# Softmax over 32,768 columns on one core: the last tile in one load and four pieces, the tile before it stored ahead

## The chip, the core and the metric

The kernel runs on one core of a Trainium2 chip. The core has engines that run side by side, each with its own instruction queue: VectorE (DVE in the profile) for maxima, sums and scalings, ScalarE (ACT) for exponentials, and SyncE (SP), which here only issues transfers. Transfers between main memory and the on-chip memory run on 16 DMA engines; a transfer is issued by SP, which uses queue q1, or by ScalarE, which uses queue q10. The metric is device time in microseconds (us). The kernel before takes 2502.16 us, the median of three runs (2502.09 to 2502.26).

## The reference

```python
scaled = logits / temperature                      # logits: 16 x 256 x 32768, float32; temperature 1.0
scaled = scaled - scaled.max(axis=-1, keepdims=True)
exp_scaled = np.exp(scaled)
return exp_scaled / exp_scaled.sum(axis=-1, keepdims=True)
```

It is a softmax over each of 4096 rows of 32,768 numbers. Input and output are 537 MB each.

## The kernel before

Each row is split into 4 parts of 8192 columns (`_SPLIT`), and a part lies on one partition. So a tile of 128 partitions holds 32 whole rows, as 128 x 8192 float32 (4 MB), and there are G = 128 tiles, 0 to 127. Six buffers of that size hold tiles in turn (`_BUFS`); everything is done in place in the buffer.

For a tile, five steps follow each other:

- `load` (L57, issued at L60 by SP): from main memory into the buffer. Tiles 0 and 127 come in two halves of 4096 columns (`cuts`, L53, `_END_CUT`), all others in one transfer.
- `peaks` (L82): VectorE takes the negated maximum of each partition (L88; with two halves, the smaller of the two at L92). `combine` (L69) then joins the four partitions of a row: two rounds of a shuffle within 32 partitions (L72) and an operation of one column (L75).
- `exps` (L101): ScalarE computes exp(x - maximum) in place and adds up each partition as it goes (L107).
- `scales` (L116): VectorE joins the sums of the four partitions (`combine` again), takes the reciprocal (L125) and multiplies the tile by it (L127).
- `store` (L64, issued at L67): back to main memory. ScalarE issues the stores of tiles 0 to 125, SP those of 126 and 127; tile 127 is stored in two halves.

The order is written out by hand (`manual_schedule`, L131 to L143); each engine executes its instructions in that order. Six loads are issued ahead. Then, for each i, `peaks(i+1)` and `exps(i+1)` come before `scales(i)` and `store(i)`, and after these the load of tile i+6 into the buffer that tile i leaves. That load has to wait until the store of tile i has landed. At the end this means: `peaks(127)` stands ahead of `scales(126)` on VectorE.

Of the kernel before, what the change touches and what calls it, by code (L numbers as in the profile page):

```python
# [1 line left out]

# [4 lines left out]


_SPLIT = 4
_BUFS = 6  # L10
_END_CUT = 4096


@with_exitstack
def kernel(
    ctx: ExitStack,
    tc: tile.TileContext,
    logits: bass.AP,
    temperature: bass.AP,
    out: bass.AP,  # L20
):
    nc = tc.nc
    inv_t = 1.0 / float(temperature)
    P = nc.NUM_PARTITIONS
    fp32 = mybir.dt.float32
    Exp = mybir.ActivationFunctionType.Exp
    X = mybir.AxisListType.X
    A = mybir.AluOpType

    xf = logits.flatten_outer_dims()  # L30
    of = out.flatten_outer_dims()
    N, V = xf.shape
    W = V // _SPLIT
    assert W * _SPLIT == V and (N * _SPLIT) % P == 0
    x = xf.rearrange("n (h v) -> (n h) v", h=_SPLIT)
    o = of.rearrange("n (h v) -> (n h) v", h=_SPLIT)
    G = N * _SPLIT // P
    R = _SPLIT.bit_length() - 1

    pool = ctx.enter_context(tc.tile_pool(name="fixed", bufs=1))  # L40
    bufs = [pool.tile([P, W], fp32, name=f"x{b}") for b in range(_BUFS)]
    stats = [
        (
            pool.tile([P, 4], fp32, name=f"pk{b}"),
            pool.tile([P, 4], fp32, name=f"sm{b}"),
            pool.tile([P, R + 1], fp32, name=f"mx{b}"),
            pool.tile([P, R + 1], fp32, name=f"su{b}"),
            pool.tile([P, 1], fp32, name=f"rs{b}"),
        )
        for b in range(4)  # L50
    ]

    def cuts(i: int) -> list[tuple[int, int]]:  # L53
        step = _END_CUT if i in (0, G - 1) else W
        return [(s, step) for s in range(0, W, step)]

    def load(i: int) -> None:  # L57
        xs = bufs[i % _BUFS]
        for s, n in cuts(i):
            nc.sync.dma_start(  # L60
                out=xs[:, s : s + n], in_=x[i * P : (i + 1) * P, s : s + n]
            )

    def store(i: int, eng) -> None:  # L64
        xs = bufs[i % _BUFS]
        for s, n in cuts(i) if i == G - 1 else [(0, W)]:
            eng.dma_start(out=o[i * P : (i + 1) * P, s : s + n], in_=xs[:, s : s + n])  # L67

    def combine(v, op) -> None:  # L69
        for j in range(R):  # L70
            mask = [k ^ (1 << j) for k in range(32)]
            nc.vector.stream_shuffle(  # L72
                out=v[:, j + 1 : j + 2], in_=v[:, j : j + 1], mask=mask
            )
            nc.vector.tensor_tensor(  # L75
                out=v[:, j + 1 : j + 2],
                in0=v[:, j : j + 1],
                in1=v[:, j + 1 : j + 2],
                op=op,
            )  # L80

    def peaks(i: int) -> None:  # L82
        xs = bufs[i % _BUFS]
        pk, _, mx, _, _ = stats[i % 4]
        cs = cuts(i)
        to = [mx[:, 0:1]] if len(cs) == 1 else [pk[:, k : k + 1] for k in range(len(cs))]
        for (s, n), t in zip(cs, to):
            nc.vector.tensor_reduce(  # L88
                out=t, in_=xs[:, s : s + n], axis=X, op=A.max, negate=True
            )  # L90
        if len(cs) > 1:
            nc.vector.tensor_reduce(  # L92
                out=mx[:, 0:1], in_=pk[:, : len(cs)], axis=X, op=A.min
            )
        combine(mx, A.min)
        if inv_t != 1.0:
            nc.vector.tensor_scalar_mul(
                out=mx[:, R : R + 1], in0=mx[:, R : R + 1], scalar1=inv_t
            )

    def exps(i: int) -> None:  # L101
        xs = bufs[i % _BUFS]
        _, sm, mx, su, _ = stats[i % 4]
        cs = cuts(i)
        to = [su[:, 0:1]] if len(cs) == 1 else [sm[:, k : k + 1] for k in range(len(cs))]
        for (s, n), t in zip(cs, to):
            nc.scalar.activation(  # L107
                out=xs[:, s : s + n],
                in_=xs[:, s : s + n],
                func=Exp,  # L110
                bias=mx[:, R : R + 1],
                scale=inv_t,
                accum_out=t,
            )

    def scales(i: int) -> None:  # L116
        xs = bufs[i % _BUFS]
        _, sm, _, su, rs = stats[i % 4]
        cs = cuts(i)
        if len(cs) > 1:  # L120
            nc.vector.tensor_reduce(  # L121
                out=su[:, 0:1], in_=sm[:, : len(cs)], axis=X, op=A.add
            )
        combine(su, A.add)
        nc.vector.reciprocal(out=rs, in_=su[:, R : R + 1])  # L125
        for s, n in cs:
            nc.vector.tensor_scalar_mul(  # L127
                out=xs[:, s : s + n], in0=xs[:, s : s + n], scalar1=rs
            )

    with tc.manual_schedule():  # L131
        for i in range(_BUFS):
            load(i)
        peaks(0)
        exps(0)
        for i in range(G):
            if i + 1 < G:
                peaks(i + 1)
                exps(i + 1)
            scales(i)  # L140
            store(i, nc.scalar if i < G - 2 else nc.sync)
            if i + _BUFS < G:
                load(i + _BUFS)  # L143


# [1 line left out]
_INS = ['logits', 'temperature']  # L147
_OUTS = [((16, 256, 32768), 'float32')]

_NUMBERS = {'temperature': 1.0}  # L150


# [26 lines left out]
```

## Time and profile before

| what | value |
|---|---|
| median of the runs | 2502.16 us |
| the profiled execution: its own time | 2501.61 us |
| its span, from the first instruction to the end | 2499.8 us |
| bytes read / written | 536.87 MB / 536.87 MB |
| VectorE idle, waiting for loads (L88, tiles in one load) | 564.1 us |
| L88, maximum of 128x8192 | 8686 ns each |
| L107, exponential, 130 instructions | 7017 ns each (mean of two sizes) |
| L127, scaling, 130 instructions | 4421 ns each (mean of two sizes) |
| 4 MB load by SP, issue to landing | 38.5 us (median of 126) |
| 4 MB store by ScalarE, issue to landing | 43.4 us (median of 126) |

The span is the profiler's; the execution's own time is 1.8 us longer and is what compares with the runs. "Landing" is the moment at which a transfer's last part has arrived. A busy engine counts only instructions that compute: waiting and issuing transfers are not in it. A line such as `ACTq L67 DMA_DIRECT2D` is the issue of a transfer, not the transfer itself. Times in windows, timeline and chain run from the start of the span.

### The profile page before, as it was taken

To read this page: it belongs to the slowest core of one execution; us is meant where nothing else is said; L and a number is where in the kernel's file an instruction comes from. 1 tells how busy PE (TensorE), PEld (TensorE's weight loads), DVE (VectorE), ACT (ScalarE), POOL (GpSimd) and SP (SyncE) were. 2 spreads that over 40 slices of the span, in tenths; PEclk is the share of its full clock that TensorE was granted. 3 is DMA by queue.
4 is the path that set the end of the run, shared out by engine and by line. 5 is a ranking of instruction groups with operands and counts; after the bars stand their busy time and mean duration, and the time that the engine had idled before them with its cause. 6 is when DMAs were issued, how large, how long until landed. Compare 5 with 4: busy or idle time off the path is not lost.

```text
span 2499.8 us, 2866 instructions
## 1 busy us (share of the span) xinstructions
DVE 1857.8 (74%) x1928; ACT 925.3 (37%) x261; POOL 0.2 (0%) x4
## 2 busy tenths in 40 slices
DVE  7877777777777777777677776777777777777765
ACT  3433433334333433334333343333433344333432
POOL 0000000000000000000000000000000000000000
DMA  9999999999999999999999999999999999999997
GB/s 411 432 435 433 433 433 434 433 433 434 434 431 434 434 433 433 434 433 432 433 435 432 433 434 433 432 433 434 433 433 433 433 432 433 435 432 434 434 431 317
DMA packets 37318, 1073.94 MB, mean 430 GB/s; under 512 B 4144, under 2 KB 4144, under 8 KB 4144
## 3 DMA queue, kind: packets, MB, share of 16 engines
q1 hardware_dynamic: 19152, 545.27, 50.6%
q10 hardware_dynamic: 18144, 528.49, 49.0%
q14 instruction: 22, 0.18, 0.0%
HBM read 536.87 MB, written 536.87 MB: 430 GB/s over the span
## 4 chain that ended last, share of the span: by engine, by line
DMA 83%; DVE 15%; ACT 1%; issue 0%; DVEq 0%; SPq 0%; ACTq 0%
DMA out_dram<-x 43%; DMA x<-in_logits_dram 40%; DVE mx L88 9%; DVE x L127 4%; ACT x L107 1%; DVE mx L72 0%; DVE su L75 0%; DVE su L72 0%; DVE mx L75 0%; DVE pk L88 0%; DVE rs L125 0%; DVEq L174 0%; SPq L60 0%; DVE su L121 0%; DVE mx L92 0%
## 5 line engine op out<-in xcount | busy, mean ns | idle before, releaser
L88 DVE TENSOR_REDUCE mx<-x 128x1 f32<-128x8192 f32 x126 | 1094.4, 8686 | 564.1 <-DMA x<-in_logits_dram 564.1
L107 ACT ACTIVATE x<-x,mx 128x8192 f32<-128x8192 f32 (+1 forms) x130 | 912.2, 7017 | 1546.5 <-DVE su L72 1469.8
L127 DVE TENSOR_SCALAR x<-x,rs 128x8192 f32<-128x8192 f32 (+1 forms) x130 | 574.5, 4421 | 4.5
L75 DVE TENSOR_TENSOR su<-su 128x1 f32<-128x1 f32 x256 | 40.9, 160 | 8.8
L75 DVE TENSOR_TENSOR mx<-mx 128x1 f32<-128x1 f32 x256 | 40.9, 160 | 8.8
L72 DVE STREAM_SHUFFLE su<-su 128x1 f32<-128x1 f32 x256 | 38.8, 151 | 0.0
L72 DVE STREAM_SHUFFLE mx<-mx 128x1 f32<-128x1 f32 x256 | 38.8, 151 | 0.0
L88 DVE TENSOR_REDUCE pk<-x 128x1 f32<-128x4096 f32 x4 | 17.7, 4418 | 18.5 <-DMA x<-in_logits_dram 18.5
L125 DVE RECIPROCAL rs<-su 128x1 f32<-128x1 f32 x128 | 21.0, 164 | 4.5
L107 ACT ACTIVATION_READ_ACCUMULATOR x<-x,mx 128x1 f32 x130 | 24.2, 186 | 0.0
L72 DVE LOAD_MASK_SELECT mx<-mx x256 | 3.6, 14 | 11.0
L72 DVE LOAD_MASK_SELECT su<-su x256 | 3.6, 14 | 5.6
L107 ACT ACT_TABLE_LOAD x1 | 1.3, 1283 | 8.2 <-DMA x<-in_logits_dram 8.2
L121 DVE TENSOR_REDUCE su<-sm 128x1 f32<-128x2 f32 x2 | 0.3, 151 | 2.2 <-ACT x L107 2.2
L92 DVE TENSOR_REDUCE mx<-pk 128x1 f32<-128x2 f32 x2 | 0.3, 155 | 0.1
L160 POOL MEMSET const-bfloat16-1.0<- 128x1 bf16 x1 | 0.1, 102 | 0.0
L160 POOL MEMSET const-uint8-127<- 128x1 uint8 x1 | 0.1, 102 | 0.0
L160 POOL MEMSET const-float32-0.0<- 128x1 f32 x1 | 0.1, 99 | 0.2 <-issue 0.2
L160 POOL MEMSET const-float32-1.0<- 128x1 f32 x1 | 0.1, 99 | 0.0
## 6 DMA issues: line engine op xcount, KB each, us to landing
x<-in_logits_dram SPq DMA_DIRECT2D x126, 4096.0 KB, 38.5
out_dram<-x ACTq DMA_DIRECT2D x126, 4096.0 KB, 43.4
x<-in_logits_dram SPq DMA_DIRECT2D x4, 2048.0 KB, 22.7
out_dram<-x SPq DMA_DIRECT2D x1, 4096.0 KB, 11.2
out_dram<-x SPq DMA_DIRECT2D x2, 2048.0 KB, 11.6
```

Source lines behind the costliest of these rows:

```text
L72: nc.vector.stream_shuffle(out=v[:, j + 1 : j + 2], in_=v[:, j : j + 1], mask=mask)
L75: nc.vector.tensor_tensor(out=v[:, j + 1 : j + 2], in0=v[:, j : j + 1], in1=v[:, j + 1 : j + 2], op=op,)
L88: nc.vector.tensor_reduce(out=t, in_=xs[:, s : s + n], axis=X, op=A.max, negate=True)
L92: nc.vector.tensor_reduce(out=mx[:, 0:1], in_=pk[:, : len(cs)], axis=X, op=A.min)
L107: nc.scalar.activation(out=xs[:, s : s + n], in_=xs[:, s : s + n], func=Exp, bias=mx[:, R : R + 1], scale=inv_t, accum_out=t,)
L121: nc.vector.tensor_reduce(out=su[:, 0:1], in_=sm[:, : len(cs)], axis=X, op=A.add)
L125: nc.vector.reciprocal(out=rs, in_=su[:, R : R + 1])
L127: nc.vector.tensor_scalar_mul(out=xs[:, s : s + n], in0=xs[:, s : s + n], scalar1=rs)
L160: nc = _bacc.Bacc("TRN2", target_bir_lowering=False, num_devices=1)
```

## The change

Four edits, all at the end of the kernel:

- Tile 127 is loaded in one transfer. Tile 0 keeps its two halves.
- `scales(126)` and `store(126)` come before anything is computed on tile 127. The loop ends at tile 126, and a new function `finish(127)` follows it.
- `finish` works in four pieces of 2048 columns. Each piece has its own maximum, and its exponential uses that maximum alone, so it need not wait for the maximum of the whole row. Afterwards the overall maximum is formed, with `combine`; a small exponential `ee` (128 x 4) gives the factor by which each piece is off; one instruction multiplies these factors by the four sums and adds them up; `combine`, the reciprocal and a small multiplication give a factor `f` for each piece. Then each piece is scaled and stored by itself: four stores of 1 MB.
- ScalarE issues all stores, those of tiles 126 and 127 included.

```diff
-_END_CUT = 4096
+_FIRST_CUT = 4096
+_LAST_CUT = 2048
...
+    last = [pool.tile([P, W // _LAST_CUT], fp32, name=nm) for nm in ("ee", "f", "tt")]
+
     def cuts(i: int) -> list[tuple[int, int]]:
-        step = _END_CUT if i in (0, G - 1) else W
+        step = {0: _FIRST_CUT, G - 1: _LAST_CUT}.get(i, W)
         return [(s, step) for s in range(0, W, step)]
 
     def load(i: int) -> None:
         xs = bufs[i % _BUFS]
-        for s, n in cuts(i):
+        for s, n in cuts(i) if i == 0 else [(0, W)]:
...
-    def store(i: int, eng) -> None:
+    def store(i: int) -> None:
         xs = bufs[i % _BUFS]
         for s, n in cuts(i) if i == G - 1 else [(0, W)]:
-            eng.dma_start(out=o[i * P : (i + 1) * P, s : s + n], in_=xs[:, s : s + n])
+            nc.scalar.dma_start(
+                out=o[i * P : (i + 1) * P, s : s + n], in_=xs[:, s : s + n]
+            )
...
+    def finish(i: int) -> None:
+        xs = bufs[i % _BUFS]
+        nm, sm, mx, su, rs = stats[i % 4]
+        ee, f, tt = last
+        cs = cuts(i)
+        for k, (s, n) in enumerate(cs):
+            nc.vector.tensor_reduce(
+                out=nm[:, k : k + 1], in_=xs[:, s : s + n], axis=X, op=A.max, negate=True
+            )
...
+            nc.scalar.activation(
+                out=xs[:, s : s + n],
+                in_=xs[:, s : s + n],
+                func=Exp,
+                bias=nm[:, k : k + 1],
+                scale=inv_t,
+                accum_out=sm[:, k : k + 1],
+            )
+        nc.vector.tensor_reduce(out=mx[:, 0:1], in_=nm, axis=X, op=A.min)
+        combine(mx, A.min)
+        nc.scalar.activation(out=ee, in_=nm, func=Exp, bias=mx[:, R : R + 1], scale=-1.0)
+        nc.vector.tensor_tensor_reduce(
+            out=tt,
+            in0=ee,
+            in1=sm,
+            scale=1.0,
+            scalar=0.0,
+            op0=A.mult,
+            op1=A.add,
+            accum_out=su[:, 0:1],
+        )
+        combine(su, A.add)
+        nc.vector.reciprocal(out=rs, in_=su[:, R : R + 1])
+        nc.vector.tensor_scalar_mul(out=f, in0=ee, scalar1=rs)
+        for k, (s, n) in enumerate(cs):
+            nc.vector.tensor_scalar_mul(
+                out=xs[:, s : s + n], in0=xs[:, s : s + n], scalar1=f[:, k : k + 1]
+            )
+
     with tc.manual_schedule():
...
-        for i in range(G):
-            if i + 1 < G:
+        for i in range(G - 1):
+            if i + 2 < G:
                 peaks(i + 1)
                 exps(i + 1)
             scales(i)
-            store(i, nc.scalar if i < G - 2 else nc.sync)
+            store(i)
             if i + _BUFS < G:
                 load(i + _BUFS)
+        finish(G - 1)
+        store(G - 1)
```

## The prediction

> **What bounds the kernel now.** I read the page first: busy times, DMA line, chain shares.
>
> ```profile
> DVE 1857.8 (74%) x1928; ACT 925.3 (37%) x261; POOL 0.2 (0%) x4
> DMA packets 37318, 1073.94 MB, mean 430 GB/s; under 512 B 4144, under 2 KB 4144, under 8 KB 4144
> DMA 83%; DVE 15%; ACT 1%; issue 0%; DVEq 0%; SPq 0%; ACTq 0%
> ```
>
> No engine is full, and 83% of the chain is transfers: the kernel moves 1,074 MB and is bound by that. The change touches only the end, so next I cut the end into stretches by window (columns: DVE busy, ACT busy, POOL busy, clock, DMA share, GB/s).
>
> ```profile
> 2300.00:2450.00 150.00, 113.16 (x120) 52.90 (x15) 0.00 (x0) 1.00 1.00 433
> 2450.00:2463.00 13.00, 7.23 (x2) 4.82 (x2) 0.00 (x0) 1.00 0.96 412
> 2463.00:2478.00 15.00, 10.39 (x16) 5.45 (x3) 0.00 (x0) 1.00 0.09 37
> 2478.00:2498.00 20.00, 5.56 (x10) 2.05 (x2) 0.00 (x0) 1.00 0.98 419
> ...
> 2470.00:2471.00 1.00, 1.00 (x1) 0.00 (x0) 0.00 (x0) 1.00 0.08 33
> ```
>
> From 2463 to 2478 the DMA engines look idle: 15 us that an early store could fill. But they are not quite idle. Full rate is 433 GB/s, or 433/16 = 27.1 GB/s for one of the 16 engines; 33 to 37 GB/s is about one engine's worth. So I asked who that is, from the time to landing of the last stores and loads (DMA issues, one window per answer), with issue times from the timeline and the chain.
>
> ```profile
> out_dram<-x ACTq DMA_DIRECT2D x1, 4096.0 KB, 38.5
> ...
> out_dram<-x ACTq DMA_DIRECT2D x1, 4096.0 KB, 33.7
> ...
> out_dram<-x ACTq DMA_DIRECT2D x1, 4096.0 KB, 23.8
> ...
> out_dram<-x SPq DMA_DIRECT2D x1, 2048.0 KB, 13.0
> ```
>
> Issued at 2414.25, 2433.57, 2452.93 and (the last half) 2485.89, these landed at 2452.75 (tile 123), 2467.27 (124), 2476.73 (125) and 2498.9 (127). A landing is complete when the last engine has done its part. Between 123 and 124, 14.52 us passed, in which one store (4.19 MB) and one half load of tile 127 (2.10 MB) landed: 6.29 MB / 16 / 14.52 us = 27.1 GB/s, exactly one engine's full rate. Between 124 and 125: 4.19 MB / 16 / 9.46 us = 27.7 GB/s. So one engine, some 10 us behind the others, never rests until 2476.73, and it alone makes the landings late. The 15 us belong to the other engines; the late one rests only from 2476.7 until the store of tile 126, issued at 2477.93, reaches it, and the two last stores then take 2498.9 - 2477.9 = 21.0 us. **The bound at the end is this one engine's remaining bytes, plus its rest.** It also explains the chain here:
>
> ```profile
> 2419.30 47.81 DMA x<-in_logits_dram
> 2467.11 0.02 issue
> 2467.14 4.43 DVE pk L88
> ```
>
> Tile 127's second half lands at 2467.1, 29.1 us after tile 126 (2438.06), where the step is 19.35. The queues' packets say why:
>
> ```profile
> q10 hardware_dynamic: 191, 5.67, 65.6%
> q1 hardware_dynamic: 193, 2.95, 34.4%
> ```
>
> From 2425 to 2445 both queues get equal numbers of packets, but those of the half loads hold half the bytes (16 KB against 32 KB), so loads get a third of the rate.
>
> **The change, part by part.**
>
> *One load for tile 127.* Packets are 32 KB again and the queues share equally, as they do all through (19.35 us a tile). The load lands at 2438.06 + 19.4 = 2457.5, not 2467.1. No bytes are saved: what the load gains, the stores beside it lose, so this is worth nothing to the late engine by itself. One SP issue (0.33 us) goes; nothing waits for it.
>
> *Tile 126 ahead.* Its exponential's accumulator is read by 2454.63 + 0.18 = 2454.8. VectorE takes 0.96 us from there to the scaling (2480.28 to 2481.24 in the same sequence), then 4.49: done at 2460.3 instead of 2477.9. The first-half maximum that filled 2452.8 to 2457.2 is gone. ScalarE issues the store at about 2460.4. What waits behind it on ScalarE is tile 127's first exponential, which needs a maximum not ready before 2462.6, so the wait costs nothing. On the late engine this store stands behind those of 124 and 125, still queued until about 2476.7. It therefore starts at 2476.7 without a rest: 4.19 MB at 433 GB/s is 9.69 us, so it lands at 2486.4 (before: 2477.93 + 11.2 = 2489.1). On the others it fills the idle 15 us, worth nothing.
>
> *Tile 127.* Four maxima of 128x2048: the rows of 8192 (8,686 ns) and 4096 (4,418) give 2.13 us per 2048, so 2.28 each, 9.1 together, from 2460.3 to 2469.4. Exponentials (3.70 for 4096, 7.12 for 8192) come to 2.0 each and keep pace; the last is read by 2471.7. The overall minimum and its combine (0.96, from 2471.59 to 2472.55) hide beside it. The small exponential `ee` has no row: between the accumulator read (0.19) and a whole 2048 piece (2.0), I take 0.3 from the line through the two sizes, so 2472.0. The multiply-and-sum has none either: between 0.16 (an add of one column) and 2.3 (a 2048 maximum); 0.3 with its gap, near the small row: 2472.3. Combine and reciprocal 0.96, `f` 0.2: 2473.5. Scaling pieces 1.2 each (4.62 for two halves): the first store issues at 2474.7, the last at 2478.3. All of it has cover: the late engine needs tile 127 only at 2486.4, 11 us after. With both upper bounds (3.7 more) and a load still landing at 2467.1 (6.8 more) it would be 2485.2, still in time. So the added small instructions cost nothing.
>
> *Four stores of 1 MB.* The two halves landed at 2483.60 + 10.3 = 2493.9 and 2498.9; from the store before (2489.1) that is 9.8 us for 4.19 MB, against 9.69 at full rate. Halving cost 0.1. For quarters I take 0.2: landing at 2486.4 + 9.9 = 2496.3. Bounds: nothing (2496.1), and 4.5 if each of the three cuts leaves the whole gap of a start on empty queues (11.2 - 9.69 = 1.5 us); 0.2 lies by the row that is nearest, a cut with another transfer queued ahead.
>
> The Trainium skill speaks against this part: "DMA: Bandwidth & Descriptors", section "Measured (HBM→SBUF, 128 partitions, SWDGE, issued from GpSimd)", gives 6.15 us and 78% of the rate to a transfer of 1 MB, and advises at least that size. Taken one after the other, four would be 24.6 us by it, an estimate that lands tile 127 at 2511.0 and makes the kernel 12 us slower. The two halves above show no such price where another transfer is queued ahead, and I go by them; no run here shows quarters yet.
>
> *All stores on ScalarE.* 126 and 127 move from SP's queue to ScalarE's. Before, both queues were empty by then; now 126 follows 125 on one queue. Five issues of 0.34 us on an idle ScalarE; SP only waits at the end.
>
> **Sum.** Last landing 2498.9 → 2496.3, 2.6 us, of which the rest on the late engine is all. Call it 2.5. The span ends 0.9 us after the last landing in both: 2497.3. The profiled execution took 2501.61, 1.8 more than its span; so 2499.1. The median shown is 0.55 above that execution: **2499.6 us**, 0.1% faster. This measurement can tell about 0.2% (5.0 us) from no change, so that counts as no change. With quarters at nothing and the faster of the two paces seen (9.46 instead of 9.69, twice) it would be 2498.9; with a gap at each cut 2503.9.
>
> **Rivals.**
> - *The idle 15 us are real for the end* (the lag dissolves, or the late engine is not one engine). For it: a DMA share of 0.09. Then tile 127's arithmetic sets the end: first issue 2474.7, and 11.2 from issue to landing of 4 MB on empty queues gives 2486, 13 us earlier: 2489. Against it: the two rates of 27.1 and 27.7 GB/s. Chance 0.09.
> - *Quarters are too small a transfer (slower).* If a quarter takes as long as a half (4.9 us), tile 127 needs 19.5 and lands at 2505.9: 2509. It decides from 3.1 us a piece (12.3 us for the four, all of the gain), and passes 0.2% at 4.3. Against it: halving cost 0.1. Chance 0.04.
> - *Nothing comes of it*: the late engine finds another gap of 2 us, at the change from 125 to 126 or from 126 to 127, so that the change does not do what it says: 2502. For it: every start on empty queues shows such a gap; against it: both stores are queued 10 us ahead. Chance 0.09.
> - My forecast: 0.78, with 2498.9 to 2503.9 as its own range.
>
> Faster by over 0.2% is the first rival, 0.09; slower the second, 0.04; the rest, 0.87, is within. The range is the forecast's, which takes in the third rival: with 0.3 below for the rounding of the views, 2498.6 to 2503.9.
>
> **What would show it.** Right: tile 127's load lands near 2457.5; the store of 126 issues near 2460.4 and lands near 2486.4, some 26 us later; first store of 127 issued near 2475, last landing near 2496.3; from 2473 on the DMA share falls towards one engine's until tile 127's pieces come, and at the very end again a stretch of some 10 us at about 30 GB/s, with the others done. Wrong: tile 126 landing 11 us after its issue, or all engines busy until the end.

## The result and the profile after

The changed kernel takes 2498.40 us, the median of 20 runs (2498.23 to 2499.61); the kernel before took 2502.10 beside it (20 runs, 2500.97 to 2503.39). The ratio is 0.9986, with a 95% interval of 0.998 to 0.9993. So it is 3.7 us faster, 0.15%, where 2.5 us were forecast: less than 0.2%, as forecast, but 0.2 us below the lower end of the range. The profiled execution took 2498.68 us, with a span of 2496.9 us.

The first three lines are from the page of the changed kernel; the others are its end cut into stretches (DVE busy, ACT busy, POOL busy, clock, DMA share, GB/s).

```profile
DVE 1858.4 (74%) x1934; ACT 926.4 (37%) x266; POOL 0.2 (0%) x4
DMA packets 37462, 1073.94 MB, mean 430 GB/s; under 512 B 4160, under 2 KB 4160, under 8 KB 4160
DMA 83%; DVE 15%; ACT 1%; issue 0%; SPq 0%; DVEq 0%; ACTq 0%
```

```profile
2450.00:2463.00 13.00, 10.86 (x11) 5.27 (x3) 0.00 (x0) 1.00 0.98 421
2463.00:2473.00 10.00, 8.17 (x21) 7.81 (x9) 0.00 (x0) 1.00 0.98 423
2473.00:2485.00 12.00, 4.45 (x4) 0.00 (x0) 0.00 (x0) 1.00 0.87 365
2485.00:2496.00 11.00, 0.00 (x0) 0.00 (x0) 0.00 (x0) 1.00 0.09 37
...
2486.00:2487.00 1.00, 0.00 (x0) 0.00 (x0) 0.00 (x0) 1.00 0.12 49
...
2492.00:2493.00 1.00, 0.00 (x0) 0.00 (x0) 0.00 (x0) 1.00 0.06 25
```

The page is all but the same. In the windows, the stretch at 0.09 and 37 GB/s has not gone: it stood at 2463 to 2478, and now it stands at 2485 to 2496, at the very end. From 2486 on no more than two engines work (0.12 is two sixteenths), and from 2490 on one alone (0.06, 25 GB/s); the others are done. The stores of tiles 126 and 127 say the same, first their issues in the timeline:

```profile
2460.05 0.34 ACTq L70 DMA_DIRECT2D out_dram<-x  x1
...
2473.90 4.02 ACTq L70 DMA_DIRECT2D out_dram<-x  x4
```

and their time to landing, for tile 126 and for the last quarter of 127 (DMA issues by window):

```profile
out_dram<-x ACTq DMA_DIRECT2D x1, 4096.0 KB, 26.0
...
out_dram<-x ACTq DMA_DIRECT2D x1, 1024.0 KB, 18.4
```

Tile 126 was issued at 2460.05 and landed 26.0 us later, at 2486.05: more than twice the 11.2 us of before, although it left 18 us sooner. The last quarter of tile 127, issued at 2477.5, landed at 2495.9. Everything waits in the queue of one engine. Tile 126's line of before, from the page, and the rest of the late engine there, a window in which no packet starts, with the same window in the changed kernel:

```profile
out_dram<-x SPq DMA_DIRECT2D x1, 4096.0 KB, 11.2
...
2476.40:2478.70 2.30, 1.50 (x1) 2.30 (x1) 0.00 (x0) 1.00 0.00 0
...
2476.40:2478.70 2.30, 1.05 (x1) 0.00 (x0) 0.00 (x0) 1.00 0.98 406
```

### The profile page after: what moved, and what is told of

It reads as the page before. It is cut to its first block, busy times and chain, and to the rows that moved or that the text cites. A ratio compares the mean times of both kernels' runs of the same rounds, so it can differ in the third digit from the quotient of the medians.

```text
span 2496.9 us, 2877 instructions
## 1 busy us (share of the span) xinstructions
DVE 1858.4 (74%) x1934; ACT 926.4 (37%) x266; POOL 0.2 (0%) x4
## 4 chain that ended last, share of the span: by engine, by line
DMA 83%; DVE 15%; ACT 1%; issue 0%; SPq 0%; DVEq 0%; ACTq 0%
DMA out_dram<-x 43%; DMA x<-in_logits_dram 40%; DVE mx L93 9%; DVE x L132 4%; ACT x L112 1%; DVE pk L142 0%; DVE su L80 0%; DVE mx L77 0%; DVE su L77 0%; DVE mx L80 0%; DVE rs L130 0%; DVE x L174 0%; ACT x L149 0%; SPq L63 0%; DVEq L223 0%
## 5 line engine op out<-in xcount | busy, mean ns | idle before, releaser
L77 DVE STREAM_SHUFFLE su<-su 128x1 f32<-128x1 f32 x256 | 38.8, 152 | 0.0
L77 DVE STREAM_SHUFFLE mx<-mx 128x1 f32<-128x1 f32 x256 | 38.8, 151 | 0.0
L93 DVE TENSOR_REDUCE pk<-x 128x1 f32<-128x4096 f32 x2 | 8.8, 4420 | 8.6 <-DMA x<-in_logits_dram 8.6
L149 ACT ACTIVATE x<-x,pk 128x2048 f32<-128x2048 f32 x4 | 8.0, 2002 | 8.0 <-DVE pk L142 7.7
L142 DVE TENSOR_REDUCE pk<-x 128x1 f32<-128x2048 f32 x4 | 8.9, 2278 | 0.0
## 6 DMA issues: line engine op xcount, KB each, us to landing
x<-in_logits_dram SPq DMA_DIRECT2D x127, 4096.0 KB, 38.5
out_dram<-x ACTq DMA_DIRECT2D x127, 4096.0 KB, 43.4
```

Source lines behind the costliest of these rows:

```text
L77: nc.vector.stream_shuffle(out=v[:, j + 1 : j + 2], in_=v[:, j : j + 1], mask=mask)
L93: nc.vector.tensor_reduce(out=t, in_=xs[:, s : s + n], axis=X, op=A.max, negate=True)
L142: nc.vector.tensor_reduce(out=nm[:, k : k + 1], in_=xs[:, s : s + n], axis=X, op=A.max, negate=True)
L149: nc.scalar.activation(out=xs[:, s : s + n], in_=xs[:, s : s + n], func=Exp, bias=nm[:, k : k + 1], scale=inv_t, accum_out=sm[:, k : k + 1],)
```

## The experiments

**Which edit does it?** Two kernels carry one edit each.

`load_only`, the kernel before with tile 127 in one load:

```diff
-        for s, n in cuts(i):
+        for s, n in cuts(i) if i == 0 else [(0, W)]:
```

> The kernel before with one edit: tile 127 loaded in one transfer. Theory (the rest of one late DMA engine before the store of tile 126 is the whole gain): the load lands near 2457, tile 126 is scaled by 2472 and its store issued before the late engine is empty (2476.7), so nearly the whole gain comes: 2498.4 to 2498.9 us, as much as the full change. Rival 1 (the idle time of all 16 engines counts): the store of tile 126 is issued 6 us sooner, so 2496. Rival 2 (part of the 3.7 us comes from the stores moved to ScalarE or from the four pieces): about 2499.5, as only the 2.5 us of the forecast are the rest.

Measured: 2498.25 us (11 runs), ratio 0.9986 (0.9978 to 0.9995).

`early_only`, the kernel before with tile 126 scaled and stored ahead of everything on tile 127:

```diff
         for i in range(G):
-            if i + 1 < G:
+            if i == G - 1:
+                peaks(i)
+                exps(i)
+            if i + 2 < G:
                 peaks(i + 1)
                 exps(i + 1)
             scales(i)
```

> The kernel before with one edit: tile 126 scaled and stored ahead of everything on tile 127; the load in two halves, tile 127 in two halves with one maximum, and the stores of 126 and 127 on SP stay. Theory: the store of tile 126 is issued near 2460.4 and the first half of tile 127 near 2483.6, both before the late engine needs them (2476.7 and 2486.4), so nearly the whole gain again: 2498.4 to 2498.9 us; the gains of the two edits do not add. Rival 1 (idle time of all engines counts): 2490 or less. Rival 2 (part of the gain from ScalarE's stores or the four pieces): about 2499.5.

Measured: 2498.43 us (11 runs), ratio 0.9987 (0.9978 to 0.9995). The three last stores of `load_only` in the timeline, and the time to landing of the first of them, tile 126:

```profile
2472.99 8.29 SPq L67 DMA_DIRECT2D out_dram<-x  x3
```

```profile
out_dram<-x SPq DMA_DIRECT2D x1, 4096.0 KB, 13.8
```

The same in `early_only`:

```profile
2460.25 25.90 SPq L67 DMA_DIRECT2D out_dram<-x  x3
```

```profile
out_dram<-x SPq DMA_DIRECT2D x1, 4096.0 KB, 26.1
```

Tile 126 was issued 12.7 us apart in the two, and landed at 2486.8 and 2486.35. Each edit alone gives the whole gain, since either one puts a store into the late engine's queue before it is empty, and more than that it can't use. Rival 1 (idle time of all engines) is out. So is rival 2: without ScalarE's stores and without the four pieces the gain is just as large, so `finish` and the move of the stores add nothing to it that these runs can tell.

**Does tile 127's arithmetic have the 11 us of cover?** Idle maxima of 128x8192 were put ahead of it, one in `delay_9` (`range(1)`), two in `delay_17`, whose edit is shown; nothing reads their result:

```diff
+    idle = pool.tile([P, 1], fp32, name="idle")
...
+        for _ in range(2):
+            nc.vector.tensor_reduce(
+                out=idle, in_=bufs[(G - 3) % _BUFS], axis=X, op=A.max, negate=True
+            )
         finish(G - 1)
```

> The changed kernel with one idle maximum of 128x8192 (8.7 us on VectorE) ahead of tile 127's work. Theory: the first store of tile 127 is issued near 2482.6 instead of 2473.9, still ahead of the late engine's need at 2486.0, so no change: 2498.4 us, within 0.5. Rival 1 (tile 127's arithmetic sets the end): 8.7 us more, 2507.

> The changed kernel with two idle maxima of 128x8192 (17.4 us on VectorE) ahead of tile 127's work. Theory: the first store is issued near 2491.3, the late engine is empty at 2486.0 and rests some 6 us, so 2504.0 to 2505.0 us. Rival 1 (tile 127's arithmetic sets the end): 17.4 us more, 2515.8.

Measured: 2498.56 us for one (10 runs; 8.7 us of added work cost 0.2, which is within the scatter; the first store of tile 127 was issued at 2482.23, ahead of tile 126's landing), and 2506.31 for two (10 runs; ratio to the kernel before 1.0017, 1.0008 to 1.0026), 1.3 above the theory's range. In `delay_17` the windows show a true rest:

```profile
2473.00:2485.00 12.00, 12.00 (x5) 4.53 (x5) 0.00 (x0) 1.00 0.10 44
2485.00:2492.00 7.00, 5.17 (x20) 4.03 (x5) 0.00 (x0) 1.00 0.00 0
2492.00:2504.00 12.00, 3.48 (x3) 0.00 (x0) 0.00 (x0) 1.00 0.84 350
```

First one engine's stretch (0.10), then nothing at all (0.00), then all engines together. The first quarter was issued at 2491.93 and landed 3.9 us later, 10.2 us after tile 126 (2460.76 + 24.8 = 2485.6), where the changed kernel needs 2.4 from one to the other: a rest of 7.8 us for 17.4 us of added work. The theory expected 6: it left out the 1.5 us that a start on empty queues takes beyond the transfer (11.2 less 9.69, for tile 126 in the kernel before).

**Why 3.7 us between medians, and 2.9 between the profiles?** The kernel before was profiled again, without any edit.

> The kernel before once more, for a second profile. Open: medians differ by 3.7 us, the two profiles by 2.9. Theory: the rest of the late engine varies by about one 32 KB packet (1.2 us) between executions, with the order in which its packets of tile 127's load and of the stores alternate. Then an execution of about 2502.2 us shows a longer step from the landing of store 125 to that of store 126 than the 12.3 us of the first profile (12.8 to 13.5), and one of about 2501.1 a shorter or equal one. Rival: the step is 12.3 in all executions and the time differs in the earlier part, so that the landing of tile 126's load moves with the time.

> As before_b, a third profile of the kernel before: theory and rival as there.

Measured: 2500.93 and 2501.48 us. The steps from the landing of store 125 to that of 126 were 12.4 and 12.5 us; the first profile's is 12.4 from the same rows, each rounded to 0.1 us (the expectation has it as 12.3). The rest did not vary here; the times differed earlier, by the landing of tile 126's load. That is what the rival expected, and neither execution was one of 2502. So the next three profiles went after one:

> The kernel before, a fourth profile. Open: why the medians differ by 3.7 us where the rest of the late engine in three profiles is 2.7 (125 to 126 in 12.3 to 12.5 us). Three profiles of before took 2500.9 to 2501.6, below the median of 2502.1. Theory of the phase: on the late engine packets of loads and stores alternate, and which queue is ahead differs by one packet between executions (in delay_17 the store of tile 122 landed 2.4 us ahead of the load of tile 126, in the other profiles 0.2 after it). The kernel before ends a fixed time after the load of tile 127, so it is later when stores are ahead; the changed one ends when the late engine's total is done, in either phase. So an execution near 2502.2 has the load of tile 126 landing near 2438.4, the store of 122 some 2.4 us ahead of it, and 125 to 126 in 13.5 or more; one near 2501.2 looks like the first three. Rival: the store lands 0.2 us after the load in a 2502.2 execution as well.

> The kernel before, a fifth profile. The theory of the phase and its rival expect here what they expect of before_d.

> The kernel before, a sixth profile. The theory of the phase and its rival expect here what they expect of before_d.

> The changed kernel, a second profile. Theory of the phase: 2498.2 to 2498.9 us in either phase, with store 125 to 126 in 9.7 us; if the stores are ahead here, the load of tile 126 lands some 1 us later than in the first profile (2437.7) and the time is no later for it. Rival: a later landing of that load is a later end by as much.

Measured: 2502.32, 2500.93, 2500.88, and 2498.27 for the changed kernel. `before_d` is the execution looked for. Its page (issues, with the median time to landing) has

```profile
x<-in_logits_dram SPq DMA_DIRECT2D x126, 4096.0 KB, 41.1
out_dram<-x ACTq DMA_DIRECT2D x126, 4096.0 KB, 40.7
```

where the other five profiles of before have 38.5 to 38.8 and 43.0 to 43.4. In the median the loads land 2.6 us later and the stores 2.7 us sooner. The last tiles show the order directly: the store of tile 122 landed at 2395.59 + 40.7 = 2436.3, 2.5 us ahead of the load of tile 126 (2438.77); in the first profile it landed 0.2 after it (2438.28 and 2438.06). The stores are ahead on the late engine, by about the time of a packet of each kind (two times 1.21 us, an estimate from 32 KB at 27.1 GB/s). At the end of `before_d`, in the timeline and then in the times to landing of the stores of 125 and 126:

```profile
2453.65 0.34 ACTq L67 DMA_DIRECT2D out_dram<-x  x1
2467.83 4.42 DVE L88 TENSOR_REDUCE pk<-x 128x1 f32<-128x4096 f32 x1 [9.89 <-DMA x<-in_logits_dram]
2478.63 0.35 SPq L67 DMA_DIRECT2D out_dram<-x  x1
```

```profile
out_dram<-x ACTq DMA_DIRECT2D x1, 4096.0 KB, 22.6
...
out_dram<-x SPq DMA_DIRECT2D x1, 4096.0 KB, 11.2
```

Tile 127 is there 0.7 us later than in the first profile (2467.1), but store 125 lands 0.5 us sooner, at 2476.25. Tile 126 lands at 2489.83: 13.6 us from one to the other, so by this sum the engine rests 3.9 us where it rested 2.7 (the step less the 9.69 of the transfer). The stretch in which no packet starts is longer by as much, 3.5 us against 2.3 in the windows:

```profile
2475.90:2479.40 3.50, 2.70 (x1) 3.50 (x3) 0.00 (x0) 1.00 0.00 0
```

The second profile of the changed kernel, `after_b`, happened to have the same order:

```profile
x<-in_logits_dram SPq DMA_DIRECT2D x127, 4096.0 KB, 41.1
out_dram<-x ACTq DMA_DIRECT2D x127, 4096.0 KB, 40.7
```

and in its timeline tile 126's maximum, which starts when the load has landed:

```profile
2438.57 8.69 DVE L93 TENSOR_REDUCE mx<-x 128x1 f32<-128x8192 f32 x1 [4.50 <-DMA x<-in_logits_dram]
```

Its tile 126 arrived 0.8 us later than in the first profile after (2437.76), and it ended 0.4 us sooner, 2498.27 against 2498.68. This is what the theory of the phase expected, and against its rival. The span of the kernel before ends 32.7 to 32.8 us after tile 127's load in all six profiles; the changed kernel ends when the late engine has moved all its bytes, in whatever order.

**Can the late engine be relieved?** In `late_15`, tile 127 is stored as 120 partitions and 8:

```diff
+            for a, b in [(0, 120), (120, P)] if i == G - 1 else [(0, P)]:
+                nc.scalar.dma_start(
+                    out=o[i * P + a : i * P + b, s : s + n], in_=xs[a:b, s : s + n]
+                )
```

> The changed kernel, with each of tile 127's four stores as two: 120 partitions and 8 partitions. Theory: the end is the late engine's queue alone. 120 partitions divide over 15 engines and not 16. If the engine left out is the late one, its last bytes are those of tile 126 (landing 2486.0) and the second latest engine sets the end, some 5.5 us earlier: 2492.5 to 2494.5 us. If another engine is left out, the late one has as much or a ninth row more per store: 2498.4 to 2499.7. Rival 1 (all engines' rate sets the end): 16/15 of 9.7 us, 0.6 more: 2499.0.

Measured: 2506.08 us (11 runs), ratio 1.0018 (1.0009 to 1.0027), slower by more than any theory had it. The issues of its last stores in the timeline, and by window the stretch in which they are under way and two of its last microseconds:

```profile
2474.05 19.70 ACTq L71 DMA_DIRECT2D out_dram<-x  x8
```

```profile
2475.00:2493.00 18.00, 2.61 (x3) 0.00 (x0) 0.00 (x0) 1.00 0.79 228
...
2495.00:2496.00 1.00, 0.00 (x0) 0.00 (x0) 0.00 (x0) 1.00 0.08 33
...
2503.00:2504.00 1.00, 0.00 (x0) 0.00 (x0) 0.00 (x0) 1.00 0.06 25
```

One engine still moves alone up to 2504, so it was not the late one that was left out. Issuing eight stores took 19.7 us, where four took 4.0, and the rate between 2475 and 2493 stayed between 139 and 311 GB/s in windows of 1 us. The engines were busy for much of that time, but moved less in it: a share of 0.79 gave 228 GB/s, where in the changed kernel 0.87 gave 365. Why this split is so slow was not found; with that the experiment says nothing on what relief of the right engine would bring.

**When does the engine fall behind?** `half_run` leaves out tiles 64 to 127:

```diff
-    G = N * _SPLIT // P
+    G = N * _SPLIT // P // 2
```

> The changed kernel on the first 64 tiles alone (tiles 64 to 127 are left out, half of the work). Theory of a slow drift (the late engine falls behind evenly over the run): the stretch at the end in which only one engine or two still move data is about half as long as in the full run (11 us from 2485 to 2496), 5 to 6 us, and the time is about 1251 to 1255 us. Rival (the late engine loses its 10 us once, at the start or at the end): the stretch stays near 10 us.

Measured: 1253.09 us (one execution).

```profile
1233.00:1244.00 11.00, 0.00 (x0) 0.00 (x0) 0.00 (x0) 1.00 0.91 384
1244.00:1250.00 6.00, 0.00 (x0) 0.00 (x0) 0.00 (x0) 1.00 0.08 34
```

The stretch in which one or two engines are left is 6 us after 64 tiles and 11 us after 128: the late engine falls behind along the way, by some 0.45% of the run, and not once at the start or the end.

## Why the prediction was right and wrong

- *The bound: one late engine's bytes and its rest.* Right. `delay_9` and `delay_17` show its cover from both sides, and the two single edits its limit.
- *One load, landing at 2457.5.* Issued at 2418.62 and landed 38.5 us later, 2457.1; this execution was 0.3 us ahead already at tile 126 (2437.76 against 2438.06). "Worth nothing to the late engine by itself" was wrong as a statement on the edit alone: it moves no bytes, but it brings tile 126's store forward to 2473, and that fills the rest by itself.
- *Tile 126 ahead: issue 2460.4, landing 2486.4.* 2460.05 and 2486.05; right, with the same 0.3.
- *Tile 127's arithmetic, first issue 2474.7, hidden.* 2473.9. The page's groups for the two operations that had no row, and the pieces:

```profile
L149 ACT ACTIVATE x<-x,pk 128x2048 f32<-128x2048 f32 x4 | 8.0, 2002 | 8.0 <-DVE pk L142 7.7
L142 DVE TENSOR_REDUCE pk<-x 128x1 f32<-128x2048 f32 x4 | 8.9, 2278 | 0.0
L160 DVE CUSTOM_DVE_ANT_0 tt<-ee,sm 128x4 f32<-128x4 f32 x1 | 0.2, 161 | 1.4 <-ACT ee L159 1.4
L159 ACT ACTIVATE ee<-pk,mx 128x4 f32<-128x4 f32 x1 | 0.3, 281 | 0.0
```

  `ee` took 0.28 us (0.3 taken) and the multiply-and-sum 0.16 (0.3 with its gap): both near the small ends of their bounds.
- *Four quarters, 9.9 us.* From 2486.05 to 2495.9, 9.9. The Trainium skill's figure for a transfer of 1 MB ("DMA: Bandwidth & Descriptors", section "Measured (HBM→SBUF, 128 partitions, SWDGE, issued from GpSimd)": 6.15 us) is not what quarters queued one behind the other cost here: each took about 2.5 us.
- *The sum, 2.6 us, called 2.5.* In the profiled executions 2501.61 became 2498.68, 2.9 us, of which 0.3 lay ahead of the last stage. Right for this execution.
- *"The median shown is 0.55 above that execution".* **This step failed.** It carried 0.55 us over to the changed kernel as if it were a constant. It was a sign that the profiled execution was not the usual one: its rest was 2.7 us, in `before_d` it is 3.9. Of the 69 times of the kernel before that stood beside these runs, 51 are above 2501.7 (median 2502.20) and 18 below it (2501.25); the changed kernel's median of 2498.40 fits both orders. From 2502.2 the gain is 3.8 us, from 2501.25 it is 2.85. Profiles of one order side by side say the same: with the stores ahead 2502.32 became 2498.27, 4.05 us, of which 0.2 lay ahead of the last stage. So the term that was mis-sized is the rest of the late engine in the usual execution: 3.9 us, where 2.6 was counted; 2502.16 less 3.9 is within 0.2 us of what was measured. That the 51 all have the stores ahead is inferred from their times: only one of the six profiled executions of the kernel before shows that order, and why they should be of the other kind so much oftener than the timed runs stays open.
- *Rivals.* The 15 us of the other engines were worth nothing, the quarters cost no more than forecast, and no second gap appeared: the DMA share is 0.87 from 2473 to 2485, and after that the late engine goes on to 2496.

## What to carry to other kernels

Where a stretch has a DMA share near 1/16 at the rate of one engine, the queues are not idle: look for the one late engine, and count the change by its rest alone. Then two edits that each fill the same rest are worth as much as one of them; here one line, the load in one transfer, brings all that the whole change brings. A profiled execution that lies outside the timed runs at hand (here 2501.61 us, against three of 2502.09 to 2502.26) is a warning: find out what differs in it before its terms are carried over. With 20 runs it turned out to lie within their scatter, which, by the times, holds two kinds of execution.

## What the runs showed of the hardware

- One of 16 DMA engines falls behind about evenly, by 6 us in 1251 and 11 us in 2497, and a second one by about half as much (two engines' rate from 2485 to 2490); seen alone, the late one moves 25 to 33 GB/s in windows of 1 us, about its share of the full rate (433/16 = 27.1). So why it falls behind is not shown. The Trainium skill ("DMA: Bandwidth & Descriptors", section "Latency and other measured facts") says that engines 7 and 15 are usually slower, and gives as its best guess, called not certain, contention from the descriptor rings of transfers issued by GpSimd. This kernel issues none there (all issues are by SP and ScalarE), and has a late engine all the same; no run here shows its number.
- Two queues with work waiting moved about equal numbers of packets, whatever their size: 193 of the loads and 191 of the stores from 2425 to 2445. With 16 KB packets against 32 KB, the loads got a third of the rate, and tile 127's second half landed 29.1 us after tile 126 instead of 19.35.
- Which queue is ahead on the late engine differs from one execution to the next, and shows in the medians of the whole run: 38.5 to 38.8 us to landing for loads and 43.0 to 43.4 for stores in nine profiles, 41.1 and 40.7 in four.
